# A written order for TensorE in the scan's rounds, with the turnings moved behind other products and into PSUM banks of their own

## The chip, the cores and the metric

The kernel runs on one core of a Trainium2 chip. The metric is the device time of one execution in microseconds (us). Engines are called as in the profile: PE is TensorE (PEld its weight loads), DVE is VectorE, ACT is ScalarE, POOL is GpSimd, SP is the sync engine, which issues most loads.

## The reference

Two layers of a diffusion backbone over 512 latent and 256 context tokens with 1024 features: windowed attention and a feed forward, then a bidirectional state-space mixer (Mamba-2) and a feed forward. The change is in the mixer. Cut to that:

```python
def ssm_project(u, w_in, conv_w, conv_b, dt_bias):
    z, xbc, dt = jnp.split(u @ w_in, [D_INNER, D_INNER + CONV_DIM], axis=-1)
    xbc = jax.nn.silu(centred_depthwise_conv(xbc, conv_w, conv_b))      # x, B, C
    dt = softplus(dt + dt_bias)
...
def ssd_chunked(xs, dt, A, Bm, Cm, h0):          # 8 groups of 4 heads, chunks of 128 tokens
    cum = cumsum(dt * A)
    decay = exp(where(tri, cum_i - cum_j, -inf))
    y_diag = (C B^T * decay) @ (x * dt)
    states = (B * to_end)^T @ (x * dt)
    h_start = scan(states, chunk_decay, h0)      # h0: the context's final state
    y_off = (C @ h_start) * exp(cum)
    return y_diag + y_off
...
def ssm_output(y, xs, z, D_skip, norm_g, w_out):
    y = (y + D_skip * xs) * silu(z)
    return rmsnorm_per_group(y) @ w_out
```

Both directions are computed. The context tokens have only their final states computed, which start the latent scans.

## The kernel before

The mixer goes group by group (8 groups). What a group needs is made by `project(g)` (L1125): the projections of x (two tiles of 128 features, latent and context tokens), B (latent and context), C and z (four token tiles). Each is a sum of 24 matmuls on TensorE: 8 slices of the features times three products of the high and low parts into which weights and tokens are split (`mm3`, L149 to L151). A latent projection has 512 columns, a context or z projection 256. A weight unit (128 x 1024) comes by an SP load (L72), is cast on ScalarE (L83) and the rest is formed on VectorE (L84); four units have room. x, B and C then go through `conv` (L1113): a copy out of PSUM and the middle tap on ScalarE (L1116, L1118), the outer taps on VectorE (L1119, L1121), silu on ScalarE (L1123). x and B are then turned on TensorE by `to_rows` (L1143, its matmuls L1146), which puts the tokens on the partitions, and copied out (L1147). The names: px, pxc are the products of x (latent, context), pb, pbc of B, pcc of C, pz of z; xf, xcf, B, bcf, C what `conv` makes of them; xT, xcT, bT, bcT the turned tiles.

The scan of a group is `ssd(g, r)` (L1200 on). `cb_step` makes C B^T (cb_ps, L1215) and two masked copies cb (L1218). `ctx_step` weighs the context's x on GpSimd (xwc, L1224) and multiplies (hc, L1232) for the start states H. `state_step` does the same for the four chunks (xw, st, L1251) and advances H, on GpSimd (L1240) and VectorE (L1242). `head_step` (four of them) loads R, the sums of one head broadcast over the partitions (L1269, 512 KB, two tiles in turn), forms their differences on VectorE (L1271, L1273), takes exp on ScalarE (L1275), weighs cb (w, L1277 on GpSimd, L1279 on VectorE), multiplies (L1281) and then has TensorE multiply (py, L1285). `out_step` (four) multiplies C by H (po, L1291), scales and adds (yo, L1295 to L1298), gates and norms (yf, L1300 to L1302) and stores to DRAM (y_mid, L1303); there are two yf tiles.

A round runs the scan of group g together with the projections of group g + 1. Seven rounds, then the last group's scan beside the output projection:

```python
    for g in range(G - 1):
        nr, steps = project(g + 1)
        table = dict(zip("CXSabcdopqr", ssd(g, r))) | dict(zip("0123wxyz", steps))
        for s_ in "C0Xac2b1Sx3ywdpzoqr":
            table[s_]()
```

This order (C cb, X context, S states, a to d heads, o to r outputs; 0 to 3 the products of x, B and C with their turnings, w to z those of z) is only what the scheduler starts from. In the rounds it is free on every engine: it runs a timeline of its own and takes from each engine's ready work. TensorE's own order is kept by hand in other stages, with `on_pe()` (L313). Each engine then executes its queue strictly in the order that results. PSUM has four tags of two banks: a for projections, b for cb, hc, st and po, d for py and for the turnings, c unused in the rounds. Ahead of the rounds, `dt_step` (L1033) forms the step sizes dt and their sums cum in a long chain of small steps over VectorE, ScalarE and TensorE (cum_ps, tot_ps, cumT, end_ps, L1072 to L1094), and stores the sums to DRAM as cum_rows, from which R is loaded.

Of the kernel before, what the change touches and what calls it, by code (L numbers as in the profile page):

```python
# [16 lines left out]
P = 128  # L17
D = 1024
# [36 lines left out]
class Weights:  # L55
    """Streams [128, 1024] weight units from DRAM and splits each into two float32r parts."""
# [71 lines left out]
def kernel(ctx: ExitStack, tc: tile.TileContext, x, c, ctx_in, c_ctx, ada_w, ada_b,  # L128
# [24 lines left out]
    # constants and vectors  # L153
# [107 lines left out]
    def rms(xt, junk, n, name):  # L261
        """1 / sqrt(mean of squares + eps) of each row"""
# [39 lines left out]
    def norm_later(*a):  # L302
        """the norm now, the turning when turn_oldest comes to it"""
# [9 lines left out]
    def on_pe():  # L313
        """from here the tensor engine keeps to the order in which its instructions are given"""
# [12 lines left out]
    class PP:  # L327
        """One PSUM pool under several tags."""
# [21 lines left out]
    # the first norm and the keys and values, as the shift and scale of each 256 features come in  # L350
# [16 lines left out]
    def h_chunk(ch):  # L367
        """features 256 * ch and on of the modulated, transposed tokens"""
# [50 lines left out]
    def rope(ps, t, nh, name):  # L419
        """rotated rows of a [128, nh*64] PSUM block"""  # L420
# [21 lines left out]
    def kv_evac(t):  # L442
        """keys (rotated) and values of token tile t out of PSUM, the keys in two float32r parts, each twice"""
# [9 lines left out]
    def k_turn(t, pools):  # L453
        """and turned"""
# [65 lines left out]
    def scores(t, b, h0, nh):  # L520
        """steps: masked scores of nh heads from h0 on of half b, query tile t, with the sink's logit behind them, and their maximum"""
# [39 lines left out]
    def weights(t, b, h0, nh):  # L561
        """their softmax weights"""
# [18 lines left out]
    def values(t, b, h0, nh):  # L581
        """their weighted values, feature on the partition: steps that turn the weights of some keys and steps that use them"""
# [45 lines left out]
    # what fills the array between the units: the coming queries and the modulation of the feed forward  # L628
# [115 lines left out]
    def add_gated(xt, ps, gate, hf, tmp, name):  # L744
        """xt[:, half] += gate * ps"""
# [379 lines left out]
    def project(g):  # L1125
# [44 lines left out]
        def both(lat, con):  # L1170
            for f_ in [lat(), con()]:
                f_()
# [296 lines left out]
```

## Time and profile before

| | us |
|---|---|
| median of 3 runs | 1976.86 (1975.98 to 1983.81) |
| span of the profiled execution | 1982.3 |
| the run nearest to it, taken as its own time | 1983.81 |
| TensorE busy (share of the span) | 1868.1 (94%) |
| TensorE weight loads | 1586.5 (80%) |
| VectorE | 1377.4 (69%) |
| ScalarE | 894.2 (45%) |
| GpSimd | 740.0 (37%) |

A busy time is the time in which an instruction of the engine runs. TensorE's matmuls overlap their neighbours and their ends are modelled, so the distance of two starts tells more than a duration. "Granted clock" is the share of TensorE's full 2.4 GHz that the chip gave it; 0.5 is 1.2 GHz. The seven rounds and the last group take roughly from 1043 to 1512 us of the span.

### The profile page before, as it was taken

The numbers are of one execution on the slowest core, as the hardware profiler recorded it, in microseconds if no ns is written. First come the engines' busy times: TensorE is split into PE (matmuls) and PEld (weight loads), VectorE is DVE, ScalarE is ACT, GpSimd is POOL, SyncE is SP. The second block draws the span as 40 slices with busy tenths as digits, with TensorE's granted clock in tenths as the row PEclk, the third lists the DMA queues.
The fourth block names the chain that finished last, engine by engine and source line by source line (L and its number), as shares of the span: only waits on it lengthen the run. The fifth ranks groups of instructions, "written<-read, shape, count | busy, mean of one in ns | idle before, by whom it ended". The sixth has DMA issues, their size and how long they took to land.

```text
span 1982.3 us, 29492 instructions
## 1 busy us (share of the span) xinstructions
PE 1868.1 (94%) x11168; PEld 1586.5 (80%) x11168; DVE 1377.4 (69%) x2359; ACT 894.2 (45%) x1607; POOL 740.0 (37%) x688
## 2 busy tenths in 40 slices
PE   6999998999999999989999999989989989999987
PEld 3777766889888888878888878777767888999877
DVE  4656655484666666687758777787777587787886
ACT  4675555344222222223556545665462454344333
POOL 1010002243333333364405545444545244535364
PEclk8999999999999999999999999999989999999989
DMA  9302137332333333344523332323243324332321
GB/s 303 119 1 86 43 98 240 121 117 86 106 107 106 107 107 107 107 132 144 162 75 110 96 87 81 112 85 105 85 157 103 113 86 123 91 107 85 107 59 70
DMA packets 226717, 214.88 MB, mean 108 GB/s; under 512 B 10352, under 2 KB 195152, under 8 KB 226576
## 3 DMA queue, kind: packets, MB, share of 16 engines
q1 hardware_dynamic: 214304, 189.56, 31.6%
q10 hardware_dynamic: 12272, 23.44, 3.4%
q8 instruction: 88, 1.44, 0.3%
q14 instruction: 53, 0.43, 0.1%
HBM read 201.27 MB, written 11.70 MB: 107 GB/s over the span
## 4 chain that ended last, share of the span: by engine, by line
PE 47%; DVE 16%; POOL 10%; DMA 10%; issue 9%; ACT 6%; ACTq 0%; POOLq 0%; DVEq 0%; SPq 0%
DVE w L107 4%; DMA R<-cum_rows 3%; PE p L149 3%; PE p L151 3%; PE p L150 3%; PE pd L149 3%; PE pd L150 2%; PE pd L151 2%; PE po L612 2%; POOL al L843 2%; DVE w L84 2%; PE ptp L596 2%; DMA raw<-in_ffn_w_gate_dram 2%; PE ada L230 2%; POOL raw L116 1%
## 5 line engine op out<-in xcount | busy, mean ns | idle before, releaser
L107 DVE TENSOR_TENSOR w<-raw,w 128x512 fp32r<-128x512 f32 x280 | 265.6, 962 | 138.8 <-ACT w L106 138.2
L106 ACT CAST w<-raw 128x512 fp32r<-128x512 f32 x280 | 166.2, 619 | 372.7 <-POOL raw L117 111.0
L149 PE MATMUL pd<-w,ah 128*128 128x512 f32 x440 | 175.1, 398 | 13.6 <-DVE y L931 9.0
L84 DVE TENSOR_TENSOR w<-raw,w 128x1024 fp32r<-128x1024 f32 (+1 forms) x117 | 152.2, 1304 | 34.0 <-ACT w L83 33.4
L150 PE MATMUL pd<-w,ah 128*128 128x512 f32 x440 | 173.5, 394 | 0.0
L83 ACT CAST w<-raw 128x1024 fp32r<-128x1024 f32 (+1 forms) x121 | 126.1, 1045 | 100.3 <-DMA raw<-in_ffn_w_down_dram 31.7
L151 PE MATMUL pd<-w,al 128*128 128x512 f32 x440 | 162.1, 394 | 4.2 <-POOL al L843 4.2
L149 PE MATMUL p<-hF_lh,w 128*128 128x256 f32 x384 | 110.7, 290 | 13.5 <-DVE ah_f L888 10.2
L149 PEld LDWEIGHTS pd<-w,ah 128*128 128x128 f32 x440 | 83.2, 189 | 35.6 <-DVE y L931 12.1
L116 POOL TENSOR_TENSOR raw<-raw 128x512 f32<-128x512 f32 x40 | 62.4, 1559 | 132.0 <-DVE w L107 126.1
L151 PE MATMUL p<-hF_lh,w 128*128 128x256 f32 x384 | 109.4, 285 | 0.0
L150 PE MATMUL p<-hF_ll,w 128*128 128x256 f32 x384 | 109.4, 286 | 0.0
L891 POOL TENSOR_TENSOR al_f<-al_f,ah_f 128x768 f32<-128x768 f32 (+1 forms) x20 | 35.2, 1759 | 186.6 <-DVE al_f L888 186.6
L151 PEld LDWEIGHTS pd<-w,al 128*128 128x128 f32 x440 | 82.6, 189 | 21.4 <-POOL al L843 4.8
L150 PEld LDWEIGHTS pd<-w,ah 128*128 128x128 f32 x440 | 83.3, 189 | 15.4
L118 POOL TENSOR_TENSOR raw<-raw,raw 128x512 f32<-128x512 f32 x40 | 56.1, 1402 | 97.6 <-DVE w L107 84.8
L843 POOL TENSOR_TENSOR al<-al_f,ah 128x768 fp32r<-128x768 f32 (+1 forms) x40 | 72.8, 1821 | 45.3 <-ACT ah L842 45.3
L888 DVE TENSOR_TENSOR al_f<-p,al_f 128x384 f32<-128x384 f32 (+1 forms) x140 | 66.1, 484 | 32.2 <-PE p L151 32.1
L149 PEld LDWEIGHTS p<-hF_lh,w 128*128 128x128 f32 x384 | 74.8, 196 | 15.5 <-DVE ah_f L888 11.4
L888 DVE TENSOR_TENSOR ah_f<-p,ah_f 128x384 f32<-128x384 f32 (+1 forms) x140 | 65.6, 484 | 26.4 <-PE p L151 23.6
L579 ACT COPY ph<-ptp 128x512 f32<-128x512 f32 (+1 forms) x96 | 52.9, 551 | 61.0 <-PE ptp L596 60.5
L149 PE MATMUL pz<-w,hD_lh 128*128 128x256 f32 x256 | 78.3, 306 | 0.0
(473 smaller groups left out, 6036.1 us busy)
## 6 DMA issues: line engine op xcount, KB each, us to landing
ar<-in_ada_w_dram SPq DMA_DIRECT2D x192, 256.0 KB, 4.3
raw<-in_ssm_w_in_dram SPq DMA_DIRECT2D x48, 512.0 KB, 4.1
raw<-in_ffn_w_gate_dram SPq DMA_DIRECT2D x44, 512.0 KB, 3.9
raw<-in_ffn_w_up_dram SPq DMA_DIRECT2D x44, 512.0 KB, 4.9
raw<-in_ffn_w_down_dram SPq DMA_DIRECT2D x44, 512.0 KB, 3.6
R<-cum_rows SPq DMA_DIRECT2D x32, 512.0 KB, 5.2
raw<-in_ssm_w_out_dram SPq DMA_DIRECT2D x16, 512.0 KB, 3.8
raw<-in_attn_w_qkv_dram SPq DMA_DIRECT2D x12, 512.0 KB, 6.0
```

The source lines that it names most:

```text
L83: nc.scalar.copy(out=hi[:, :n], in_=t[:, :n])
L84: (eng or nc.vector).tensor_tensor(out=lo[:, :n], in0=t[:, :n], in1=hi[:, :n].bitcast(F32), op=ALU.subtract)
L106: nc.scalar.copy(out=hi, in_=src)
L107: nc.vector.tensor_tensor(out=lo, in0=src, in1=hi.bitcast(F32), op=ALU.subtract)
L116: eng.tensor_tensor(out=a22, in0=a21, in1=a22, op=ALU.add)
L118: eng.tensor_tensor(out=a11, in0=a22, in1=a11, op=ALU.subtract)
L149: nc.tensor.matmul(ps, lhsT=ah, rhs=bh, start=start, stop=False)
L150: nc.tensor.matmul(ps, lhsT=ah, rhs=bl, start=False, stop=False)
L151: nc.tensor.matmul(ps, lhsT=al, rhs=bh, start=False, stop=stop)
L579: nc.scalar.copy(out=dst, in_=src)
L843: (nc.vector if (layer, m) in ((0, 18), (1, 20)) else nc.gpsimd).tensor_tensor(out=al, in0=u_, in1=ah.bitcast(F32), op=ALU.subtract)
L888: nc.vector.tensor_tensor(out=to, in0=ps, in1=other, op=ALU.add)
```

## The change

The matmuls, their shapes and the numbers they compute stay. The steps are cut finer and named: the weighing (xw, w03, w12), the matmuls that use it (X, s03, s12), the head's weights (e0 to e3) and its matmuls (h0 to h3), a product (x0, k0, b, ...; k is x of the context) and its turning (Tx0, Tk0, Tb, ...). A table `ROUND` orders them, and within a round TensorE keeps that order. The other engines' orders are still the scheduler's. The turnings go to PSUM tag c. Comments were removed throughout; the rest of the kernel is the same.

```diff
         def to_rows(src, n, dst, name, eng):
-            tp = psum["d"].tile([P, 512], F32, name=name)
+            tp = psum["c"].tile([P, 512], F32, name=name)
...
-        steps = [lambda: x_step(0), lambda: x_step(1), b_step, c_step] + [lambda t=t: z_step(t) for t in range(NL)]
...
+        steps = {"x0": lambda: x_gemm(0), "x1": lambda: x_gemm(1), "k0": lambda: xc_gemm(0), "k1": lambda: xc_gemm(1),
+                 "b": b_gemm, "bc": bc_gemm, "c": c_gemm} | {f"z{t}": lambda t=t: z_step(t) for t in range(NL)}
...
+        def ctx_weigh():
+            for u in range(NC_):
+                wt[NL + u] = weighted(r["xc"][:, u, :], NL + u, (0, 1), f"xwc_{g}_{u}")
...
+        def state_weigh(*ts):
+            for t in ts:
+                wt[t] = weighted(r["xt"][:, t, :], t, dirs_of[t], f"xw_{g}_{t}")
...
-        def head_step(h):
...
+        def head_weigh(h):
...
             nc.vector.tensor_tensor(out=w, in0=e, in1=w, op=ALU.mult)
+            ws[h] = w
+
+        def head_step(h):
+            col, w = 4 * g + h, ws[h]
...
+    ROUND = ("cb e0 xw x0 X w03 k0 e1 x1 Tx0 Tk0 s03 w12 k1 h0 e2 s12 b Tx1 Tk1 h1 e3 bc h2 c Tb z0 Tbc h3 z1 o0 o1 z2 o2 z3 o3").split()
     for g in range(G - 1):
+        es_m[0] = on_pe()
         nr, steps = project(g + 1)
-        table = dict(zip("CXSabcdopqr", ssd(g, r))) | dict(zip("0123wxyz", steps))
-        for s_ in "C0Xac2b1Sx3ywdpzoqr":
-            table[s_]()
+        own, turns = ssd(g, r), {}
+        for s_ in ROUND:
+            if s_[0] == "T":
+                turns.pop(s_[1:])()
+            elif s_ in own:
+                own[s_]()
+            else:
+                turns[s_] = steps[s_]()
         r = nr
+        es_m[0].close()
...
-    for s_ in mine:
-        s_()
+    for s_ in "cb xw X e0 h0 e1 h1 w03 s03 w12 s12 e2 h2 e3 h3 o0 o1 o2 o3".split():
+        mine[s_]()
```

What this makes of the queues is shown at three places. The first is TensorE in the fifth round, where the context part of the next group's x is turned (xcT). Before, it stood within the product of B for the context, behind px, pxc and pb:

```order
L150 MATMUL pbc_12258<-hD_cl,w_12222 128x256
L1146 MATMUL xcT_0_12163<-ident,xcf_0_12125 128x128 x2
L151 MATMUL pbc_12258<-hD_ch,w_12223 128x256
L149 MATMUL pbc_12258<-hD_ch,w_12222 128x256
L150 MATMUL pbc_12258<-hD_cl,w_12222 128x256
```

Now both turnings stand together behind the second tile's latent product, and the state products and pxc stand behind them:

```order
L151 MATMUL px_1_12223<-hD_lh,w_12220 128x512
L1146 MATMUL xT_0_12254<-ident,xf_0_12122 128x128 x4
L1146 MATMUL xcT_0_12260<-ident,xcf_0_12169 128x128 x2
L1252 MATMUL st_0_12264<-xw_0_12165,bt_11487 128x256
L1252 MATMUL st_3_12266<-xw_3_12167,bt_11487 128x256
L149 MATMUL pxc_1_12279<-hD_ch,w_12219 128x256
```

The turnings are full products behind their own product, and the four outputs, which before ended the round in a row, now stand before and between z2 and z3.

The second place is VectorE in the same round, from the first head's weights to the context part of x (xcf). Before:

```order
L84 TENSOR_TENSOR w_12439<-raw_12436,w_12438 128x1024
L1281 TENSOR_TENSOR w_0_12186<-R_0_12178,w_0_12186 128x512
L1302 TENSOR_SCALAR yf_3_12060<-yf_3_12060,rstd_y_3_12065 128x256
L1119 SCALAR_TENSOR_TENSOR xcf_0_12125<-u_256_12151,vecC,xcf_0_12125 128x255
L1281 TENSOR_TENSOR w_2_12207<-R_2_12199,w_2_12207 128x512
L1121 SCALAR_TENSOR_TENSOR xcf_0_12125<-u_256_12151,vecC,xcf_0_12125 128x255
L1147 COPY xt_12069<-xT_0_12157 128x4x128
L1271 TENSOR_TENSOR R_1_12299<-R_1_12299,cum 128x512
```

Now the differences of the third and fourth head (R_2, R_3) and a weight's rest (w_12495) stand before the last step of xcf:

```order
L1277 TENSOR_TENSOR w_0_12109<-R_0_12101,w_0_12109 128x512
L1302 TENSOR_SCALAR yf_3_12071<-yf_3_12071,rstd_y_3_12076 128x256
L1277 TENSOR_TENSOR w_1_12209<-R_1_12201,w_1_12209 128x512
L1119 SCALAR_TENSOR_TENSOR xf_0_12122<-u_512_12154,vecC,xf_0_12122 128x511
L1121 SCALAR_TENSOR_TENSOR xf_0_12122<-u_512_12154,vecC,xf_0_12122 128x511
L1267 TENSOR_TENSOR R_2_12316<-R_2_12316,cum 128x512
L1269 SCALAR_TENSOR_TENSOR R_2_12316<-R_2_12316,cum 128x128 x4
L84 TENSOR_TENSOR w_12495<-raw_12492,w_12494 128x1024
L1267 TENSOR_TENSOR R_3_12396<-R_3_12396,cum 128x512
L1119 SCALAR_TENSOR_TENSOR xcf_0_12169<-u_256_12195,vecC,xcf_0_12169 128x255
L1269 SCALAR_TENSOR_TENSOR R_3_12396<-R_3_12396,cum 128x128 x4
L1121 SCALAR_TENSOR_TENSOR xcf_0_12169<-u_256_12195,vecC,xcf_0_12169 128x255
```

R_2 takes the tile that R_0 leaves with the first row here. On ScalarE, in the same place, the two exp and a table load now stand between the middle tap of xcf and its silu:

```order
L1118 ACTIVATE xcf_0_12169<-u_256_12195,vecB,vecC 128x256
L1271 ACT_TABLE_LOAD
L1271 ACTIVATE R_2_12316<-R_2_12316 128x512
L1271 ACTIVATE R_3_12396<-R_3_12396 128x512
L1123 ACT_TABLE_LOAD
L1123 ACTIVATE xcf_0_12169<-xcf_0_12169 128x256
```

Before, the silu of xcf followed the copies of H without a table load. Over a whole round ScalarE loads a table 6 times now, 8 times before. Rounds two to six have the same order on every engine.

The third place is TensorE ahead of the first round, in `dt_step`. Before, the next group's px and 14 of its pxc products filled the chain:

```order
L149 MATMUL px_0_9714<-hD_lh,w_9710 128x512
L1072 MATMUL cum_ps<-dt_a,scst 128x4x32 x2
L1077 MATMUL tot_ps<-dt_a,scst 128x256
L150 MATMUL px_0_9714<-hD_ll,w_9710 128x512
L151 MATMUL px_0_9714<-hD_lh,w_9711 128x512
```

Now those products belong to the round's block behind cb_ps, and the chain follows the last product of the first group at once:

```order
L151 MATMUL pbc_9654<-hD_ch,w_9575 128x256
L1072 MATMUL cum_ps<-dt_a,scst 128x4x32 x2
L1077 MATMUL tot_ps<-dt_a,scst 128x256
L1094 MATMUL cumT<-ident,cum 64x128 x4
L1083 MATMUL end_ps<-dt_a,scst 128x4x32
```

## Rows read from the trace of the kernel before

**Rows 1.** Waits of TensorE in rounds two to seven: us in total, times, longest.
```profile
PE xcT L1146 <- ACT xcf L1123: 8.9, 7, 1.9
PE bT L1146 <- ACT B L1123: 8.3, 5, 1.9
PE st L1251 <- DVE H L1242: 7.4, 4, 2.3
```
**Rows 2.** Windows, same stretch: length, PE, PEld, DVE, ACT, POOL busy; clock, DMA, GB/s.
```profile
1092.91:1471.06 378.15, 351.81 (x2054) 294.92 (x2053) 282.77 (x520) 210.74 (x344) 173.35 (x217) 0.97 0.33 99
```
**Rows 3.** Timeline of TensorE, one round: start, duration, [idle before <- releaser].
```profile
1344.39 1.02 PE L1291 MATMUL po<-H,C 128*128 128x512 f32 x2
...
1367.63 0.44 PE L1146 MATMUL xcT<-ident,xcf 128*128 128x128 f32 x2 [1.79 <-ACT xcf L1123]
```
**Rows 4.** Timeline of VectorE, the same round.
```profile
1355.94 1.28 DVE L1218 TENSOR_TENSOR cb<-cb_ps,scst 128x512 f32<-128x512 f32 x2
...
1359.40 1.49 DVE L1279 SCALAR_TENSOR_TENSOR w<-cb,dt,w 128x128 f32<-128x128 f32 x4
...
1362.88 1.22 DVE L84 TENSOR_TENSOR w<-raw,w 128x1024 fp32r<-128x1024 f32 x1
1364.02 0.68 DVE L1281 TENSOR_TENSOR w<-R,w 128x512 f32<-128x512 f32 x1
...
1366.60 0.47 DVE L1121 SCALAR_TENSOR_TENSOR xcf<-u,vecC,xcf 128x255 f32<-128x255 f32 x1
```
**Rows 5.** Tile R in rounds two to seven: ns min/median/max; last the load's us.
```profile
L1273 DVE SCALAR_TENSOR_TENSOR R<-R,cum x96: 332/340/1136, 1116.7 to 1456.3; 128x128 f32<-128x128 f32 x96
...
L1271 DVE TENSOR_TENSOR R<-R,cum x24: 676/691/1480, 1116.0 to 1453.4; 128x512 f32<-128x512 f32 x24
...
DMA to landing us min/median/max: 4.7/5.2/6.0
```
**Rows 6.** Timeline of ScalarE, the same round as rows 3.
```profile
1367.16 0.42 ACT L1123 ACTIVATE xcf<-xcf 128x256 f32<-128x256 f32 x1 [4.06 <-DVE xcf L1121]
...
1378.10 1.28 ACT L1275 ACT_TABLE_LOAD   x1
1379.39 0.63 ACT L1275 ACTIVATE R<-R 128x512 f32<-128x512 f32 x1
```
**Rows 7.** The chain that ended last, in the same round: start, us.
```profile
1348.98 4.12 DMA y_mid<-yf
```
**Rows 8.** Tile y_mid in rounds two to seven: landing of its stores.
```profile
DMA to landing us min/median/max: 1.9/2.3/5.7
```
**Rows 9.** Groups of TensorE by line, rounds two to seven: busy us, mean ns, idle.
```profile
L1232 PE MATMUL hc<-xwc,bc 128*128 128x512 f32 x24 | 11.3, 592 | 0.0
...
L1215 PE MATMUL cb_ps<-C,B 128*128 128x128 f32 x48 | 6.3, 274 | 0.0
```
**Rows 10.** Timeline of TensorE ahead of the first round.
```profile
1032.46 0.39 PE L149 MATMUL px<-hD_lh,w 128*128 128x512 f32 x1
1032.69 0.39 PE L150 MATMUL px<-hD_ll,w 128*128 128x512 f32 x1
...
1036.89 0.61 PE L1072 MATMUL cum_ps<-dt_a,scst 128*128 128x128 f32 x4
...
1038.92 0.28 PE L149 MATMUL pxc<-hD_ch,w 128*128 128x256 f32 x1
1039.04 0.28 PE L150 MATMUL pxc<-hD_cl,w 128*128 128x256 f32 x1
...
1043.14 1.06 PE L1215 MATMUL cb_ps<-C,B 128*128 128x128 f32 x8
```
**Rows 11.** Timeline of TensorE in the last feed forward, at a long wait.
```profile
1918.87 0.58 PE L149 MATMUL p<-hF_lh,w 128*128 128x256 f32 x1 [7.56 <-DVE ah_f L888]
```
**Rows 12.** Windows behind that wait, and behind a wait of 1.9 us of xcT.
```profile
1918.90:1924.80 5.90, 5.90 (x28) 5.90 (x29) 5.64 (x9) 1.10 (x2) 5.66 (x4) 0.51 0.01 3
...
1304.00:1313.00 9.00, 8.06 (x48) 6.80 (x48) 6.66 (x12) 6.03 (x9) 2.85 (x2) 1.00 0.37 121
```

More of the change, by code (lines that the diff above doesn't have):

```diff
@@ L1168, in bc_gemm, with c_gemm @@
             return lambda: to_rows(xcf, NC_, r["bc"], f"bcT_{g}", nc.scalar.copy)
-        def both(lat, con):
-            for f_ in [lat(), con()]:
-                f_()
-        def x_step(i):
-            both(lambda: x_gemm(i), lambda: xc_gemm(i))
-        def b_step():
-            both(b_gemm, bc_gemm)
-        def c_step():
+        def c_gemm():
             conv(fm_gemm(fm_unit(2 * DIN + 1024 + g * P), False, f"pcc_{g}"), L, 24 + g, r["C"])
@@ L1195, in z_step @@
             nc.scalar.activation(out=r["z"][:, t, :], in_=ps[:, 0:256], func=AF.Silu)
-        steps = [lambda: x_step(0), lambda: x_step(1), b_step, c_step] + [lambda t=t: z_step(t) for t in range(NL)]
-        r["alone"] = [lambda: x_gemm(0)(), lambda: x_gemm(1)(), lambda: b_gemm()(), lambda: xc_gemm(0)(), lambda: xc_gemm(1)(), lambda: bc_gemm()()]
+        steps = {"x0": lambda: x_gemm(0), "x1": lambda: x_gemm(1), "k0": lambda: xc_gemm(0), "k1": lambda: xc_gemm(1),
+                 "b": b_gemm, "bc": bc_gemm, "c": c_gemm} | {f"z{t}": lambda t=t: z_step(t) for t in range(NL)}
+        r["alone"] = [lambda: x_gemm(0)(), lambda: x_gemm(1)(), lambda: b_gemm()(), lambda: xc_gemm(0)(), lambda: xc_gemm(1)(), lambda: bc_gemm()(),
+                      c_gemm] + [lambda t=t: z_step(t) for t in range(NL)]
         return r, steps
@@ L1226, in weighted @@
             return xw
+        wt = {}
+        def ctx_weigh():
+            for u in range(NC_):
+                wt[NL + u] = weighted(r["xc"][:, u, :], NL + u, (0, 1), f"xwc_{g}_{u}")
         def ctx_step():
@@ L1230, in ctx_step @@
             for u in range(NC_):
-                xw = weighted(r["xc"][:, u, :], NL + u, (0, 1), f"xwc_{g}_{u}")
-                nc.tensor.matmul(ps, lhsT=r["bc"][:, u, :], rhs=xw.rearrange("p d f -> p (d f)"), start=u == 0, stop=u == NC_ - 1)
+                nc.tensor.matmul(ps, lhsT=r["bc"][:, u, :], rhs=wt[NL + u].rearrange("p d f -> p (d f)"), start=u == 0, stop=u == NC_ - 1)
             nc.scalar.copy(out=H[:, 0, 0, :], in_=ps[:, 0:256])
@@ L1242, in advance, with state_step @@
             nc.vector.tensor_tensor(out=dst, in0=ps_half, in1=dst, op=ALU.add)
-        def state_step():
-            S = {}
-            for t in (0, 3, 1, 2):
-                dirs = (0,) if t == 0 else (1,) if t == NL - 1 else (0, 1)
-                xw = weighted(r["xt"][:, t, :], t, dirs, f"xw_{g}_{t}")
-                lo, hi = 256 * dirs[0], 256 * dirs[-1] + 256
-                ps = psum["b"].tile([P, 512], F32, name=f"st_{g}_{t}")
-                nc.tensor.matmul(ps[:, lo:hi], lhsT=r["bt"][:, t, :], rhs=xw.rearrange("p d f -> p (d f)")[:, lo:hi], start=True, stop=True)
-                S[t] = ps
-                if t == 0:
-                    advance(ps[:, 0:256], 0, 0)
-                elif t == 3:
-                    advance(ps[:, 256:512], 3, 1)
-            advance(S[1][:, 0:256], 1, 0)
-            advance(S[2][:, 256:512], 2, 1)
-            advance(S[2][:, 0:256], 2, 0)
-            advance(S[1][:, 256:512], 1, 1)
+        dirs_of = {0: (0,), 1: (0, 1), 2: (0, 1), 3: (1,)}
+        S = {}
+        def state_weigh(*ts):
+            for t in ts:
+                wt[t] = weighted(r["xt"][:, t, :], t, dirs_of[t], f"xw_{g}_{t}")
+        def state_step(*ts):
+            for t in ts:
+                lo, hi = 256 * dirs_of[t][0], 256 * dirs_of[t][-1] + 256
+                S[t] = psum["b"].tile([P, 512], F32, name=f"st_{g}_{t}")
+                nc.tensor.matmul(S[t][:, lo:hi], lhsT=r["bt"][:, t, :], rhs=wt[t].rearrange("p d f -> p (d f)")[:, lo:hi], start=True, stop=True)
+            for t, d in ((0, 0), (3, 1)) if 0 in ts else ((1, 0), (2, 1), (2, 0), (1, 1)):
+                advance(S[t][:, 256 * d:256 * d + 256], t, d)
         y = sp.tile([P, NL, 4, 64], F32, tag="y", name=f"y_{g}", bufs=1)
-        def head_step(h):
+        ws = {}
+        def head_weigh(h):
             col = 4 * g + h
@@ L1303, in out_step @@
             nc.scalar.dma_start(out=y_mid[t][:, g * 256:(g + 1) * 256], in_=yf)
-        return [cb_step, ctx_step, state_step] + [lambda h=h: head_step(h) for h in range(4)] + [lambda t=t: out_step(t) for t in range(NL)]
+        return {"cb": cb_step, "xw": ctx_weigh, "X": ctx_step, "w03": lambda: state_weigh(0, 3), "w12": lambda: state_weigh(1, 2),
+                "s03": lambda: state_step(0, 3), "s12": lambda: state_step(1, 2)} | \
+            {f"e{h}": lambda h=h: head_weigh(h) for h in range(4)} | {f"h{h}": lambda h=h: head_step(h) for h in range(4)} | \
+            {f"o{t}": lambda t=t: out_step(t) for t in range(NL)}
     r, steps = project(0)
     es_m[0].close()
-    start = dict(zip("xybpqr3zwuv", r["alone"] + steps[3:])) | {"T": turn_oldest, "D": dt_step}
+    start = dict(zip("xybpqr3zwuv", r["alone"])) | {"T": turn_oldest, "D": dt_step}
     for s_ in "TTzpwquvD3ybxr":
```

## The prediction

> **What bounds the kernel now.** The waits of TensorE come first, because it is busy 94% of the span and so each of its gaps counts. In rounds two to seven it waits in three places: for the silu of the context part of x, for that of B, and for the advanced states; in most rounds each costs between 1 and 2 us [rows 1]. The windows give the size of the prize. The stretch from the end of the first round's products to that of the seventh's is 378.15 us, or 63.0 a round. TensorE is idle 378.15 - 351.81 = 26.3 us of it, 4.4 a round, and the granted clock of 0.97 takes another 3%, some 11 us, 1.9 a round [rows 2]. What is left, 56.8 us a round, is matmuls one behind the other. If every wait went, six rounds would save at most 6 x 6.2 = 37 us. VectorE, with 282.8 us of 378, is not the bound on the whole, but it works through its queue in order, so the reader has to see what stands ahead of the step that TensorE waits for.
>
> **How a wait arises.** The timelines of one round show it. Call T the end of the last z product of a round, 1344.39 [rows 3]. VectorE comes to the masks cb at T + 11.5, finishes xcf at T + 22.7 [rows 4], ScalarE's silu starts at T + 22.8 [rows 6], and TensorE turns at T + 23.2, having waited 1.79 [rows 3]. TensorE had px, pxc, pb, more than half of pbc and four outputs to do until then.
>
> **The change part by part.**
>
> *TensorE's arrival.* Now, behind T, there are one po (1.0 us [rows 3]), cb (6.3/6 = 1.05) and hc (11.3/6 = 1.9 [rows 9]), px and the second px (24 x 0.23 = 5.5 each, by the distance of starts), pxc (24 x 0.12 = 2.9 [rows 10]) and the first turning, taken as 0.4. Together 18.2: TensorE stands at xcT at T + 18.2, and as it keeps its order it can't go on with anything else.
>
> *VectorE's and ScalarE's arrival.* (1) Two outputs now come before z2, so less is left behind T: two splits of a weight at 1.2 and two steps of about 0.7 [rows 4], 3.8 by their durations and 3.5 as they overlap. If the store that frees the yf tile takes 4.1 us [rows 7] instead of the usual 2.3 [rows 8], it is 5. (2) The masks 1.3, two yf steps 1.4, w of two heads 1.5 and 1.1, w times R 0.7: 5.5 to 5.9 [rows 4]. That frees the tile of R_0 at T + 9 to T + 10.9. (3) Only then is R_2 loaded, 5.2 us, at least 4.7 [rows 5]: T + 14.2 to T + 16.1. The convolution of xf fits under it. (4) In VectorE's queue R_2 (0.69 + 4 x 0.34 = 2.05), a split (1.2), R_3 (2.05) and two steps of xcf (0.5 and 0.5, up to 0.8) [rows 4, 5] stand ahead of the silu: 6.0, T + 20.2 to T + 22.1. (5) ScalarE does exp of R_3 (0.6), loads a table (1.28) and then the silu (0.4) [rows 6], of which some 0.4 lies beside VectorE's last step: 1.9. So the turning can start at T + 22.1 to T + 24.0, no sooner than now, since what was gained at (1) is lost to R_2, R_3, the split and the table. TensorE waits 3.9 to 5.8 us; I take 5, the middle, as the load's median and either store are equally near.
>
> *The old waits.* The three of rows 1 go: the state products now have s03 to s12 apart by a whole pxc and py, and the turnings of B and of the second x have more than a product between. The new wait delays them further, so I count nothing for them, save in the last rival. Minus 4.4 a round.
>
> *The clock.* A wait of 7.56 [rows 11] was followed by 5.9 us at half clock, 3 us lost; one of 1.9 us by none [rows 12]. For 5 us I take 2.0, nearer to the long one; bounds 0 and 3. Before, 1.9 a round were lost.
>
> The Trainium skill (TensorE: Matmul & The Clock Gate, section "Why this matters for your kernels") tells to leave no longer idle gap between bursts of matmuls in the middle of a kernel, as the clock falls to half behind one. That speaks against this change, which puts one gap in place of three; rows 11 and 12 agree with it. Were the clock kept instead, the same sum would give 1981.
>
> *A round.* 56.8 + 5.0 + 2.0 = 63.8 against 63.0: +0.8, six times +5 us.
>
> *Ahead of the first round.* The 24 px and 14 pxc products that filled the chain of the step sizes now come behind it: 24 x 0.23 + 14 x 0.12 = 7.2 us. The chain itself starts earlier, as cum_ps can follow the first group's last product, by up to 1036.89 - 1032.46 less two turnings = 3.6, and ends a little faster (a table load and two exp that TensorE now waits for, against 2.8 us of products between cum_ps and cb [rows 10]). I take +3; bounds 0, all covered, and +7.2, none.
>
> *The first round.* R_0 and R_1 can't be there early, as their sums are only just stored, so four sets of differences and two loads stand ahead of xcf's silu, not two and one. I estimate 3 us more of waiting than in the others. Here there were hardly any waits to save. +8; bounds +3 and +12.
>
> *Costs counted as nothing.* Own banks for the turnings: no wait of rows 1 is for a bank of tag d, so nothing is gained there. The finer steps of weighing on GpSimd are the same instructions (173 us busy of 378 [rows 2]). Two table loads fewer a round free 2.6 us of ScalarE, which is busy 210.7 of 378 [rows 2] and only matters at the silu above. The last group's scan and all behind it keep their work.
>
> *The sum.* 5 + 3 + 8 = +16 us. The profiled execution, taken as 1983.8, would become 1999.8; it stands 7 above the median, 1976.9, so against that the forecast is **1993 us**.
>
> The Trainium skill (ScalarE: Activation LUTs, section "What ACT_TABLE_LOAD costs") puts a switch of tables at 1283 ns and a drain of some 1380 behind it, 2.66 us in all. Rows 6 show the next exp 1.29 us behind the start of the load, so the measured price is used; by the page the silu would come 1.4 later and the time be about 2001.
>
> **The rivals.**
>
> *VectorE is in time (faster).* If what stands ahead of xcf took 4 to 6 us less (the differences hidden under the products, the yf steps earlier), the new wait would be 0 to 2 and the clock would stay. A round is then 56.8 to 58.8, six save 37 to 25, less 3 and 3 at the start: 1946 to 1958, say 1952. For it: the three old waits are truly moved out of the way. Against it: the load of R_2 alone, behind w times R, takes 4.7 at least [rows 5], and its place in the queue is fixed. The point: VectorE has to free R_0 by about T + 5, while the masks alone can't start before cb at T + 2. Chance 0.20.
>
> *One wait for three (no difference).* The wait is near 3.9, and the clock holds as behind 1.9 us [rows 12]. A round is 60.7, six save 14, the start costs 3 + 6: 1972. For it: the two ends of the walk are equally supported. Against it: the gap is twice as long as any that rows 1 show. Chance 0.27.
>
> *The forecast*, 1993, chance 0.38; with its parts between 1983 and 2002.
>
> *A second wait behind the first (slower still).* VectorE's next load of R is released by the third head's w, which the first wait delays; B's convolution stands behind it in the queue. If that comes later than the product c covers, the turning of B waits as now, some 2 us a round more: 65.8 a round, +17, with 3 and 8: 2005. For it: the same pattern of a load ahead of a convolution. Against it: c adds 5.5 us of cover. Chance 0.15.
>
> That the change does nothing is no rival: the order of TensorE is plainly another.
>
> **How the numbers follow.** The likeliest is the forecast, 1993. The range runs from 1957, where the faster case has a wait of 2 us, to 2010, the last rival with a little more loss of clock; the forecast's own is 1983 to 2002. About 0.5%, 10 us, is what a measurement of this kernel can tell from no change. Slower by more: nearly all of the forecast's 0.38 and the last rival's 0.15, less 0.02: 0.51. Within: 0.28. Faster: 0.21.
>
> **What would show it.** In the changed profile, TensorE should wait once a round at xcT for the silu of xcf, 4 to 6 us, with half clock behind it; the waits for states and for B should be gone; the distance between ends of the last z product should be near 63.8. VectorE should show a wait for the load of R just ahead of it. cb of the first round should start near 1039, with a gap between tot_ps and end_ps. The forecast is wrong if xcT waits under 2 us: then VectorE's queue was shorter than its rows say. It is wrong the other way if bT or a bank of tag a is waited for as well.

## The result, and the profile after

The changed kernel took 2012.6 us (median of 4, 2005.7 to 2017.0), the kernel before 1980.3 beside it: a ratio of 1.0168, interval 1.0138 to 1.0197, so 27 to 39 us slower. The forecast was 1993, its range ended at 2010. The sign and the place of the wait in the rounds came out as forecast; the size, 32 us by the medians, was twice the sum's 16.

| us | before | after | difference |
|---|---|---|---|
| span of the profiled execution | 1982.3 | 2003.9 | +21.6 |
| up to the dt product, where the programs' orders are still the same | 997.8 | 992.1 | -5.7 |
| from there to the first round's last z product | 95.1 | 107.2 | +12.2 |
| six rounds, z product to z product | 378.15 | 388.68 | +10.5 |
| behind that | 511.3 | 515.9 | +4.6 |

The 5.7 us of the second line are scatter between two executions, since nothing has changed up to there. Without it the profiles differ by 27.3 us. The other 5 of the 32 us between the medians are not placed by this table: the profiled execution of the changed kernel is the fastest of its four (2005.7), that of the kernel before (1983.8) is the third of its four.

The third and the last line are not quite like for like. The outputs did not all stand behind the last z product before, as the part on the change has it: one stood ahead of it and three behind, as TensorE's rows of the round of [rows 3] show (T is 1344.39 there):

```profile
1340.69 1.02 PE L1291 MATMUL po<-H,C 128*128 128x512 f32 x2
1344.39 1.02 PE L1291 MATMUL po<-H,C 128*128 128x512 f32 x2
1345.49 1.02 PE L1291 MATMUL po<-H,C 128*128 128x512 f32 x2
1350.78 1.02 PE L1291 MATMUL po<-H,C 128*128 128x512 f32 x2
```

Now three stand ahead and one behind. Two outputs, about 1.7 us of TensorE, have so passed from the last line to the third. By the same work the start lost about 10 us and what lies behind the rounds about 6.5.

TensorE's waits in the six rounds of the changed kernel (us in total, times, longest), all that there are; they answer to [rows 1]:

```profile
PE xcT L1146 <- ACT xcf L1123: 37.3, 6, 6.6
PE pz L149 <- ACT z L1185: 0.7, 3, 0.3
```

The three old waits are gone and one has come, 6.2 us a round, at the place forecast. The windows (length, PE, PEld, DVE, ACT, POOL busy; clock, DMA, GB/s) show the six rounds, then the 3.5 us behind one such wait, then the rest of that round:

```profile
1099.36:1488.04 388.68, 350.34 (x2053) 294.06 (x2053) 282.25 (x519) 195.85 (x333) 158.18 (x217) 0.95 0.33 96
...
1317.70:1321.20 3.50, 3.50 (x13) 3.14 (x14) 1.42 (x3) 1.51 (x3) 1.87 (x4) 0.50 0.02 5
1321.20:1358.38 37.18, 37.08 (x242) 31.94 (x242) 25.70 (x49) 19.94 (x33) 14.58 (x20) 1.00 0.25 74
```

Against [rows 2] the rounds lose 10.5 us. Behind the wait the granted clock is at 1.2 GHz for 3.5 us, which costs 1.75. Now one round, with T = 1293.74, the end of its last z product (the prediction's T is the start of the output behind it, 0.2 us sooner). TensorE's timeline, with the last z product, the output, the turning of the latent x and then of the context's:

```profile
1293.46 0.28 PE L151 MATMUL pz<-w,hD_ll 128*128 128x256 f32 x1
1293.58 1.02 PE L1291 MATMUL po<-H,C 128*128 128x512 f32 x2
...
1311.05 0.60 PE L1146 MATMUL xT<-ident,xf 128*128 128x128 f32 x4
1317.70 0.69 PE L1146 MATMUL xcT<-ident,xcf 128*128 128x128 f32 x2 [6.05 <-ACT xcf L1123]
```

VectorE's, which TensorE waits for through ScalarE:

```profile
1297.75 1.27 DVE L1210 TENSOR_TENSOR cb<-cb_ps,scst 128x512 f32<-128x512 f32 x2
...
1301.17 3.76 DVE L1275 SCALAR_TENSOR_TENSOR w<-cb,dt,w 128x128 f32<-128x128 f32 x8
1304.86 0.68 DVE L1277 TENSOR_TENSOR w<-R,w 128x512 f32<-128x512 f32 x1
...
1310.21 0.69 DVE L1267 TENSOR_TENSOR R<-R,cum 128x512 f32<-128x512 f32 x1 [2.13 <-DMA R<-cum_rows]
1310.94 1.14 DVE L1269 SCALAR_TENSOR_TENSOR R<-R,cum 128x128 f32<-128x128 f32 x4
1311.99 1.22 DVE L84 TENSOR_TENSOR w<-raw,w 128x1024 fp32r<-128x1024 f32 x1
...
1315.18 0.47 DVE L1121 SCALAR_TENSOR_TENSOR xcf<-u,vecC,xcf 128x255 f32<-128x255 f32 x1
```

And ScalarE's end of the chain:

```profile
1315.29 0.63 ACT L1271 ACTIVATE R<-R 128x512 f32<-128x512 f32 x1 [2.55 <-DVE R L1269]
1315.94 1.28 ACT L1123 ACT_TABLE_LOAD   x1
1317.23 0.42 ACT L1123 ACTIVATE xcf<-xcf 128x256 f32<-128x256 f32 x1
```

TensorE is ready at T + 17.9. VectorE frees R_0 at T + 11.8, stands for 2.1 us until R_2 has landed at T + 16.5, and reaches the end of xcf at T + 21.9; a table load later the turning starts at T + 24.0.

### The profile page after: what moved, and what is told of

The parts are those of the page before. It is cut to its first block, busy times and chain, and to the rows that moved or that the text cites. A ratio compares the mean times of both kernels' runs of the same rounds, so it can differ in the third digit from the quotient of the medians.

```text
span 2003.9 us, 29492 instructions
## 1 busy us (share of the span) xinstructions
PE 1867.4 (93%) x11168; PEld 1583.5 (79%) x11168; DVE 1377.0 (69%) x2359; ACT 888.5 (44%) x1603; POOL 715.9 (36%) x688
## 4 chain that ended last, share of the span: by engine, by line
PE 42%; DVE 19%; DMA 11%; POOL 11%; issue 10%; ACT 6%; ACTq 0%; POOLq 0%; DVEq 0%; SPq 0%
DMA R<-cum_rows 5%; DVE w L107 4%; PE po L612 2%; PE pd L149 2%; PE pd L150 2%; DVE w L84 2%; POOL al L843 2%; PE ptp L596 2%; PE p L149 2%; PE pd L151 2%; PE p L151 2%; PE p L150 2%; DMA raw<-in_ffn_w_gate_dram 2%; DMA raw<-in_ffn_w_down_dram 2%; DVE R L1269 2%
## 5 line engine op out<-in xcount | busy, mean ns | idle before, releaser
L118 POOL TENSOR_TENSOR raw<-raw,raw 128x512 f32<-128x512 f32 x40 | 56.5, 1412 | 95.2 <-DVE w L107 83.2
L149 PEld LDWEIGHTS p<-hF_lh,w 128*128 128x128 f32 x384 | 74.0, 194 | 16.1 <-DVE ah_f L888 11.8
L888 DVE TENSOR_TENSOR ah_f<-p,ah_f 128x384 f32<-128x384 f32 (+1 forms) x140 | 65.5, 483 | 25.3 <-PE p L151 22.4
```

The source lines that it names most:

```text
L118: eng.tensor_tensor(out=a11, in0=a22, in1=a11, op=ALU.subtract)
L149: nc.tensor.matmul(ps, lhsT=ah, rhs=bh, start=start, stop=False)
L888: nc.vector.tensor_tensor(out=to, in0=ps, in1=other, op=ALU.add)
```

## The experiments

The theory: the differences of R_2 and R_3, with the load that they wait for, stand ahead of xcf on VectorE, and that delay is what the change costs. The rivals: TensorE's rigid order by itself; a general lateness of VectorE that only passes from place to place; the banks. Edits are to the changed kernel unless it says otherwise. Ratios are to the kernel before, beside 1.0168 of the changed kernel.

### What stands ahead of xcf

**R_2 and R_3 tied behind xcf** (`e2_diff_behind`). On VectorE alone, `conv` keeps its last step and the differences queue behind it; TensorE's order is untouched:

```diff
+            elif s_ in ("e2", "e3"):
+                with tc.issue_after(tap_of["k0"].ins):
+                    own[s_]()
```

> The changed kernel with TensorE's table as it is; only the differences of the third and fourth head (R_2, R_3) are tied behind the last step of xcf on VectorE, so that the silu of xcf comes ahead of the two exp and of the table load. Theory (what stands ahead of xcf in VectorE's and ScalarE's queues makes the wait): the silu can run at T + 18 instead of T + 23.5, TensorE waits at most 1 us at xcT, and the time falls by 35 to 48, to 1965 to 1977. Rival (the wait comes from something else on the way, or the differences that come later make the heads late): the wait stays over 3 us, or py of the third head waits by 2 us or more a round, and the time is above 1990.

Measured: 1.0016 (1.0002 to 1.0029), 1986.9 us: 26 us less than the changed kernel by the medians, 30 by the ratios, where 35 to 48 were forecast. A round is 59.9 us, and the granted clock in the six rounds is 1.00, where it was 0.95. Its waits, and VectorE and ScalarE in one round with T = 1285.80:

```profile
PE xcT L1148 <- ACT xcf L1125: 10.1, 12, 0.9
PE st L1254 <- DVE H L1241: 2.1, 6, 0.5
```

```profile
1303.51 0.48 DVE L1123 SCALAR_TENSOR_TENSOR xcf<-u,vecC,xcf 128x255 f32<-128x255 f32 x1
1303.91 1.28 DVE L1269 TENSOR_TENSOR R<-R,cum 128x512 f32<-128x512 f32 x2
```

```profile
1304.09 0.42 ACT L1125 ACTIVATE xcf<-xcf 128x256 f32<-128x256 f32 x1 [1.36 <-DVE xcf L1123]
```

The silu starts at T + 18.3, where T + 23.5 was. The wait is 0.8 us, twice a round, and no head pays for the later differences: TensorE waits for none of the heads' weights. So the theory holds in the rounds: they are now 3 us shorter than before the change, yet the whole is no faster. What eats that lies at the two ends. The next table has the stretches of the result's table, here with the end of a last z product as the mark in every kernel, and the part of the last stretch up to the output projection's first product (so). Its last three kernels are described below:

| us | dt product to first round's last z | six rounds | behind that | of it, up to so |
|---|---|---|---|---|
| before | 95.2 | 378.2 | 511.1 | 20.6 |
| changed | 107.2 | 388.7 | 515.9 | 26.1 |
| `e2_diff_behind` | 105.9 | 359.5 | 521.0 | 29.9 |
| `f2_first_free` | 102.4 | 359.5 | 517.5 | 26.0 |
| `f3_last_dep` | 105.8 | 360.5 | 515.5 | 24.2 |
| `h1_together` | 101.1 | 359.8 | 514.2 | 23.4 |

**Only R_3 tied** (`h3_only_r3`), with `("e3",)` in place of `("e2", "e3")`:

> The changed kernel with only R_3 tied behind the last step of xcf on VectorE; R_2, with the wait for its load, and the split stay ahead of it, and on ScalarE the exp of R_2 with a table load on either side. Theory of the sum in the prediction (queue and load both count): 2.0 us of R_3 and the exp of R_3 go from the chain, the silu runs some 3 us sooner, the wait of xcT falls from 6.2 to about 3, a round from 64.8 to between 61 and 62.5, the time to 1988 to 1998. Rival (the load of R_2 alone holds the round): the wait stays over 5 us and the time within 6 us of the changed kernel.

Measured: 1.0147 (1.0125 to 1.0169), 2011.3 us, where 1988 to 1998 were forecast; the wait is 4.65 us a round, a round 64.0. ScalarE shows why the 3 us became 1.5:

```profile
1314.56 0.63 ACT L1273 ACTIVATE R<-R 128x512 f32<-128x512 f32 x1 [0.41 <-DVE R L1271]
1316.65 1.28 ACT L1125 ACT_TABLE_LOAD   x1 [1.46 <-DVE xcf L1123]
1317.95 0.42 ACT L1125 ACTIVATE xcf<-xcf 128x256 f32<-128x256 f32 x1
```

The table load came only when xcf was there, so its 1.28 us stood in the chain in full although ScalarE was idle ahead of it. VectorE was done with xcf only 1.5 us sooner behind T, and ScalarE gave 0.2 on top. The edit also parts the two exp, so ScalarE now loads a table 8 times a round instead of 6. A miss in size: half of the queue ahead does not give half of the gain. What is left ahead, the load, R_2, the split and the table, still makes 4.65 us of wait; which of them makes how much is not shown. In `e2_diff_behind` the split stands ahead of xcf as well, and the wait there is 0.8.

**Three tiles for R** (`e3_three_r`), `RB = 3` for `RB = 2`:

> The changed kernel with three tiles for R instead of two, so that no load of R waits for w times R of the same round; the order of VectorE is the same with the heads shifted by one, two sets of differences, a split and the table load still stand ahead of the silu of xcf. Theory of the sum in the prediction (the load is one part of the chain, the queue behind it the other): VectorE's wait of 2.1 us for the load goes and the wait of xcT falls from 6.2 to about 4.0; with the clock 2.1 to 3 us a round, 1990 to 1998. Rival (the load alone makes the wait, all else would be in time): xcT waits under 1.5 us and the time falls below 1980.

Measured: 1.0208 (1.0181 to 1.0236), 2023.1 us, not told apart from the changed kernel; xcT waits 6.4 us a round. The edit did not do what was meant. VectorE and the SP queue:

```profile
1313.71 0.68 DVE L1277 TENSOR_TENSOR w<-R,w 128x512 f32<-128x512 f32 x1
...
1319.89 0.69 DVE L1267 TENSOR_TENSOR R<-R,cum 128x512 f32<-128x512 f32 x1 [2.94 <-DMA R<-cum_rows]
```

```profile
1314.42 1.23 SPq L1265 DMA_DIRECT2D R<-cum_rows  x2
```

The next load still takes the tile that w times R_0 leaves, only it is R_3's now, and the scheduler puts its differences in the same place, just behind the load's landing. Another tile shifts the names; it takes neither the load nor the differences away from there. What the load alone costs stays open.

### Where TensorE stands

**xcT behind the product of B** (`e1_xct_late`), nothing else moved on VectorE:

```diff
-... x1 Tx0 Tk0 s03 w12 k1 h0 e2 s12 b Tx1 Tk1 ...
+... x1 Tx0 s03 w12 k1 h0 e2 s12 b Tk0 Tx1 Tk1 ...
```

> The changed kernel with one edit: the turning of the first context part (xcT_0) moves in TensorE's table from behind the second x product to behind the product of B; VectorE's and ScalarE's orders in the rounds stay as they are. Theory (the single wait for the silu of xcf, 6.2 us a round with half clock behind it, is what the change costs): TensorE comes to this turning some 12 us later, the wait goes, and a round takes 57 to 59 us instead of 64.8; six rounds and the first win 38 to 50, so about 1965 to 1975, some 0.5% faster than the kernel before. Rival (VectorE is late on the whole, and the wait only passes on to the next place where TensorE needs it, the state products, py or the turnings of the second x): other waits of 3 us or more a round appear, a round takes 61 to 63, and the time is 1985 to 2000.

Measured: 1.0116 (1.0089 to 1.0143), 2005.0 us, a round 63.2: by the ratios 10 of the 33 us come back, and the intervals still touch. The rival was right in kind, though it expected 1985 to 2000; the wait passed on:

```profile
PE xcT L1146 <- ACT xc L1147: 13.5, 6, 3.3
PE st L1252 <- DVE H L1239: 12.7, 6, 3.7
```

The second context turning waits until ScalarE has copied the first out of its bank; that copy stands behind a silu of xcf for which ScalarE stands 4 us until VectorE is done. The states wait for VectorE directly. So it is not TensorE's place alone: what VectorE is late with is waited for elsewhere.

**The scheduler's order again** (`f1_free`), `ExitStack()` in place of `on_pe()` in the rounds:

> The changed kernel with TensorE's order in the rounds given back to the scheduler, which starts from the same table: the split steps and the banks stay, and VectorE's order from cb to xcf is the same as in the changed kernel, with R_2, the split and R_3 ahead of xcf. On TensorE the two state products and 15 of the 24 products of the second pxc now come ahead of xcT_0, so TensorE stands there 3.2 us later. Theory (what costs is how much sooner TensorE comes to xcT_0 than the silu of xcf): the wait falls from 6.2 to about 3, a round from 64.8 to about 61, the time to 1983 to 1995. Rival (the given order itself, by other places than this one, or by what it does ahead of the first round, is the loss): the time falls below 1978 though xcT_0 still waits some 3 us.

Measured: 1.0153 (1.0127 to 1.0178), 2008.9 us, not told apart from the changed kernel. The wait is 5.1 us, a round 64.5. TensorE came to xcT 2.6 us later behind T, but the silu came 1.6 later too. So the loss does not need the given order: it comes with the finer steps and their sequence, from which the scheduler makes VectorE's order. No run parts the finer steps from their sequence.

**Turnings behind the states and py** (`f4_turns`), on top of the tied kernel:

```diff
-... x1 Tx0 Tk0 s03 w12 ... b Tx1 Tk1 h1 e3 ...
+... x1 Tx0 s03 Tk0 w12 ... b Tx1 h1 Tk1 e3 ...
```

> The kernel of the experiment that ties R_2 and R_3 behind xcf, with one further edit of TensorE's table: the turning of the first context part comes behind the first two state products, that of the second behind py of the second head. Theory (twelve waits of 0.8 us at xcT, 1.6 us a round, are left): 1 to 1.5 us a round less, 59.9 to about 58.6, and 6 to 10 us in all, 1977 to 1981. Rival (the wait passes on to the state products, which then wait for xw or H): a round stays over 59.5 and the time within 3 us of that experiment.

Measured: 1.0030 (1.0013 to 1.0047), 1987.6 us, a round 60.2, the same as the tied kernel within the intervals. The rival: xcT waits no more, bT (8.5 us in six rounds) and the states (7.3) do.

### The banks

**Banks alone, in the kernel before** (`e4_banks_only`), `psum["c"]` for `psum["d"]` in `to_rows`:

> The kernel before with one edit: the turnings of x, B and their context parts go to the PSUM banks of tag c instead of those of tag d; TensorE's order in the rounds is the scheduler's. Theory (no wait of the kernel before is for a bank of tag d, so the banks are worth nothing): within 8 us of the kernel before. Rival (turnings and py hinder each other in the two banks of tag d, and the banks are the part of the change that helps): 1950 to 1970, and if the other banks are what hurts, 1990 or more.

Measured: 0.9963 (0.9945 to 0.9981), 1976.0 us beside 1983.9: 7 to 8 us faster, at the edge of the theory's 8 and short of the rival. A round falls to 60.1 us and the granted clock in the rounds rises from 0.97 to 1.00. But the scheduler's order moved with the banks (xcT no longer waits), so this is not the banks' doing alone.

**Tag d again, in the changed kernel** (`h2_bank_d`), where the order stays:

> The changed kernel with one edit: the turnings go back to the PSUM banks of tag d, which py uses; the order of TensorE in the rounds and of VectorE up to xcf stays. Theory (in the given order the turnings stand a product away from py, and the round is set by the silu of xcf): within 5 us of the changed kernel, 2007 to 2018. Rival (the banks are worth here what they were worth in the kernel before, 8 us by the runs and up to 16 in the rounds of the trace): 2020 to 2030.

Measured: 1.0260 (1.0238 to 1.0282), 2033.8 us, beyond even the rival: by the ratios (1.0260 less 1.0168) the banks are worth 18 us here. A round is 67.7 us, 2.9 more than with tag c; the wait at xcT is the same 6.3, and two waits of py for a turning's bank have come, 1.8 a round:

```profile
PE py L1285 <- ACT bt L1147: 7.6, 6, 1.4
PE py L1285 <- DVE xt L1147: 3.4, 6, 0.6
```

**Tag d in the kernel with the three edits** that is described under Together (`i2_ties_bank_d`):

> The kernel with the three edits together, with the turnings back in tag d. Theory (py comes right behind a turning that holds its bank in three places of the given order, and waits until ScalarE or VectorE has copied it out, 1.8 us a round in the changed kernel with tag d): a round 61.5 to 63.5 instead of 60.0 and 1985 to 1996. Rival (the banks only counted because VectorE and ScalarE were late behind the wait of xcT): a round under 60.8 and 1974 to 1979.

Measured: 1.0133 (1.0118 to 1.0148), 2010.7 us; by the ratios 35 us above the same kernel with tag c (0.9957), a round 65.5. Theory and rival both fell short. TensorE's waits, and one of them beside VectorE:

```profile
PE py L1287 <- DVE xt L1149: 32.9, 12, 4.9
```

```profile
1332.65 0.69 DVE L1269 TENSOR_TENSOR R<-R,cum 128x512 f32<-128x512 f32 x1 [4.09 <-DMA R<-cum_rows]
1333.26 0.68 DVE L1149 COPY xt<-xT 128x512 f32<-128x512 f32 x1
```

It is the same trap a second time: the copy that frees the bank stands behind a difference that waits 4.1 us for its load. With tag d py needs that bank; with tag c only a later turning does.

### The two ends

**First round left to the scheduler** (`f2_first_free`), tied kernel with `on_pe() if g else ExitStack()`:

> The kernel of the experiment that ties R_2 and R_3 behind xcf, with one further edit: the first round is left to the scheduler on TensorE. Products of px and pxc can then fill the chain of the step sizes again, as in the kernel before. Theory of the prediction's sum (the bare chain and the waits of the first round cost some 6 us or more against the kernel before): the stretch from cum_ps to the second round's cb gets 4 to 7 us shorter, 1980 to 1983. Rival (the chain ends as much sooner as the products come later): within 2 us of that experiment.

Measured: 0.9991 (0.9979 to 1.0003), 1981.2 us, less than the tied kernel by 5.7 us (medians) or 5 (ratios); from cum_ps to the second cb 63.8 us instead of 71.0. The time is as the theory has it, the reason only in part, as the table shows. cum_ps itself starts 3.7 us later behind the dt product (39.2 instead of 35.5), since products now stand ahead of it, so the start as a whole gains 3.5. Another 3.5 lie behind the rounds, where the edit changed TensorE's order too: in the tied kernel the products of the third head of the last group stand ahead of the output projection, here they stand behind its start.

**R_2 and R_3 of the last group tied behind yA_ll** (`f3_last_dep`), on the tied kernel:

```diff
+        if s_ in ("e2", "e3"):
+            with tc.issue_after(last_yt[0].ins):
+                mine[s_]()
```

> The kernel of the experiment that ties R_2 and R_3 behind xcf, with one further edit in the last group's scan: there R_2 and R_3 are tied behind the last step of yA_ll on VectorE, which the output projection waits for. Theory (in the last group too the differences that wait for a load stand ahead of what TensorE waits for): the first product of the output projection starts 3 to 6 us sooner behind the last z product than the 29.9 us of that experiment, and the time falls by as much, to 1981 to 1984. Rival (GpSimd's weighing and the masks set the time there, or the heads that come later are waited for instead): within 2 us of that experiment, or slower.

Measured: 0.9986 (0.9970 to 1.0001), 1979.4 us, less than the tied kernel by 7.5 us (medians) or 6 (ratios), and a little under the theory's 1981. The output projection starts 24.2 us behind the last z product instead of 29.9. A part of this is again the third head's products, which stand behind that start here. Among kernels with the same products in that stretch it is 22.9 to 24.2 us with the tie (`f3_last_dep`, `h1_together`, `i1_ties_free`, `i2_ties_bank_d`) and 25.2 to 26.9 without (the changed kernel, `e3_three_r`, `f1_free`, `f2_first_free`), so in the profiles the tie takes some 2.5 us off that stretch. The cleanest pair is `h1_together` (below) against `f2_first_free`, which differ in this tie alone: 7 us by the runs, 3.3 behind the rounds in the profiles. In the changed kernel the chain of waits shows the same differences there:

```profile
1502.23 0.60 DVE w L1277
1502.86 5.06 DMA R<-cum_rows
1508.02 0.69 DVE R L1267
...
1513.53 0.61 DVE yA_ll L1328
1514.18 0.50 PE so L149
```

### Together

**The three edits in one kernel** (`h1_together`):

> The changed kernel with the three edits of the experiments before together: R_2 and R_3 tied behind xcf in the rounds, the first round left to the scheduler on TensorE, R_2 and R_3 of the last group tied behind yA_ll. Theory (the three places are apart, so their gains add): 1986.9 less 5.7 less 7.5, about 1974, between 1970 and 1977, some 0.5% faster than the kernel before. Rival (what one frees, the next wait takes): 1978 to 1981, no better than the best of them alone.

Measured: 0.9957 (0.9943 to 0.9972), 1973.9 us. By the medians the gains add to 0.2 us, by the ratios to 1; so close a fit is in part luck, as the runs of each kernel spread over 4 to 10 us. It is faster than both kernels, by 0.4% than the one before.

**The same with TensorE's order left to the scheduler in every round** (`i1_ties_free`):

> The kernel with the three edits together, except that TensorE's order is the scheduler's in all rounds, not in the first alone; R_2 and R_3 stay tied behind xcf and behind yA_ll. TensorE's order then differs by the context turning, which comes behind the two state products and 4 products of the second pxc, and by turnings and py put between products. Theory (the given order by itself is worth nothing; what counts is what stands ahead of xcf on VectorE): 1970 to 1978, a round 59.5 to 60.3, like the 60.0 of the kernel with the three edits. Rival (the given order keeps waits away that the scheduler's order has): 1980 or more. Rival on the other side (the scheduler's order, free of the 0.8 us waits at xcT, gains them): below 1969.

Measured: 0.9955 (0.9939 to 0.9972), 1976.3 us, a round 60.1: in rounds two to seven the given order by itself is worth nothing that can be measured, with the ties or without them.

**Kernel before with banks and the last group's tie** (`h4_banks_last`):

> The kernel before with the turnings in tag c, as in the experiment on the banks alone, and R_2 and R_3 of the last group tied behind the last step of yA_ll. Theory (what the ties gained in the last group of the changed kernel they gain here too): the first product of the output projection starts 3 to 5 us sooner behind the last z product than the 25.1 us of that experiment, and the time is 1968 to 1973. Rival (here the differences do not stand in the way, or the last heads come too late): within 2 us of 1976, or slower.

Measured: 0.9949 (0.9931 to 0.9967), 1972.5 us; the output projection starts 22.9 us behind the last z product, 2.2 sooner, where 3 to 5 were forecast. The smallest ratio of all, but the intervals of this, the banks alone and the two kernels above overlap; the tie's own gain here is not settled.

## Why the prediction was wrong

The wait in the rounds was foreseen, with its place and its cause. Two terms of the sum failed. The silu's arrival was taken too early, which made the six rounds cost 10.5 us instead of 5. And the last group's scan and all behind it were put at nothing; there the profiles differ by 4.6 us, some 6.5 by the same work. The profiles lie 11 us above the sum's 16, and 10 of these are in the two. The start came out near its forecast. Term by term:

- **The place and the old waits**: right. One wait a round, at xcT, with R_2's load, R_3, a split and a table load ahead of it, and no wait of [rows 1] left. The place was not found by luck; the walk of VectorE's queue led to it.
- **TensorE's arrival**: T + 18.2 forecast, T + 17.9 measured.
- **The silu's arrival**: this term was mis-sized. Step (2) was to take 5.5 to 5.9 us and free R_0 at T + 9 to T + 10.9; it took 7.8, from T + 4.0 to T + 11.8. The eight steps of w took 3.76 us, not 2.6, and one yf step 1.27, not 0.4 to 0.7 (the last section says beside what). The load behind it was 0.5 us and the queue of step (4) 0.6 us shorter than reckoned, which by luck gave half of this back. The turning came at the walk's latest end, T + 24.0. The wait is 6.2 us where I took 5, outside the bounds of 3.9 to 5.8.
- **The clock**: 2.0 a round forecast, 1.75 measured in the round shown.
- **A round**: 63.8 forecast, 64.8 measured, so the six rounds cost +10.5 instead of +5.
- **Start and first round**: +3 and +8 forecast, together +12.2 measured, about 10 by the same work; here xcT waits 5.25 us, too. In the tied kernel, leaving the first round to the scheduler (`f2_first_free`) took 3.5 of it away.
- **"The last group's scan and all behind it keep their work"**: the second step that failed. The work is the same, its order on VectorE is not. The output projection starts 26.1 us behind the last z product instead of 20.6, with two outputs less to do, and behind its start nothing is lost. The chain of waits goes through the differences of R there, and the tie behind yA_ll takes 2.5 us of the stretch away in the profiles and 7 us of the time in the two runs that differ in it alone. It was not run on the changed kernel by itself, so how much of the loss there is its part stays open. Had the walk of one round's queue been repeated for the last group, the sum would have held a term for it.
- **"Own banks: nothing is gained"**: wrong. The three waits of [rows 1] name no bank of tag d, but the same view has a fourth line that they leave out, py behind the copy of a turning (`PE py L1285 <- DVE xt L1147: 1.6, 1, 1.6`). That was once in six rounds of the scheduler's old order. In the new order the banks are worth 18 us: the change without them is 2.6% slower than before, 51 us. The sum did not suffer by it, as it has no wait of py in it.
- **What does the harm**: the prediction had both TensorE's rigid order ("it can't go on with anything else") and what stands ahead of xcf on VectorE. The runs that gave the order back (`f1_free`, `i1_ties_free`) show that in rounds two to seven the freedom is worth nothing; in the first round it takes 3.5 us away (`f2_first_free`). The harm in the rounds comes from where the finer steps and their sequence put R_2 and R_3 on VectorE: with these two tied behind xcf, and TensorE's table untouched, 30 of the 33 us come back by the ratios.

## What to carry to other kernels

When the order of one engine is rewritten, read the queues of the others again: an instruction that waits for a load, placed just ahead of a short step that TensorE needs, costs its wait and all that follows it. Cure the queue that is late (here one tie on VectorE) rather than move the engine that waits; the runs that moved TensorE's turnings show that a moved wait comes back elsewhere. And test parts of a change apart: here the change without the new banks costs 51 us and the banks win 18 of them back, and the whole showed only the difference.

## What the runs showed of the hardware that was not expected

**VectorE's short steps stretch beside GpSimd.** The two engines in the same round, VectorE's yf step and GpSimd's steps:

```profile
1299.98 1.27 DVE L1300 TENSOR_TENSOR yf<-y,z 128x256 f32<-128x256 f32 x1
```

```profile
1299.87 2.29 POOL L1273 TENSOR_TENSOR w<-cb,dt 128x512 f32<-128x512 f32 x2
...
1303.03 1.23 POOL L1216 TENSOR_TENSOR xw<-xt,dtw 128x256 f32<-128x256 f32 x2
```

The yf step is at its shortest 0.41 us; here it took 1.27. Of the 96 steps of w in the six rounds, 0.34 us in the median, 18 took longer than 0.45: in every round the same three, 1.13, 0.76 and 0.70. The first ends 0.15 us behind GpSimd's step of w, the other two lie beside its step of xw. Over these four steps VectorE loses 0.86 + 0.79 + 0.42 + 0.36 = 2.4 us, which is more than the 0.9 us by which R_0 came free later than my latest estimate. The Trainium skill (SBUF — State Buffer, section "SBUF: two separate sides") says that GpSimd and a VectorE instruction with two inputs in SBUF take a shared pair of ports in turn, and that whoever comes second is blocked for the whole instruction of the other. The rows agree with that. Transfers can't be the reason for all of it: the DMA share (the last number but one) is full beside the yf step, but nothing beside the steps of 0.76 and 0.70:

```profile
1299.98:1301.25 1.27, 1.27 (x6) 0.94 (x5) 1.27 (x3) 0.00 (x0) 1.27 (x2) 1.00 1.02 303
1303.03:1304.41 1.38, 1.38 (x15) 1.38 (x13) 1.38 (x4) 0.14 (x1) 1.23 (x3) 1.00 0.00 0
```

No run moved GpSimd's steps, so the cause is not shown.

**A table load did not run ahead of the data of the activation behind it.** In `h3_only_r3` the load ahead of the silu began only when xcf had come, after 1.46 us in which ScalarE was idle (the rows stand at that run). In the same profile a semaphore instruction of the silu's line stands just ahead of the load, near 1316.6. So it can be the program's order, with the wait put ahead of the load, and nothing of the chip; no run parts the two.
